# A decoder trunk in fp32r on one core: three weight pieces shared out anew, and a last half cut at 512, 384 and 128 columns

## The chip, the cores and the metric

The kernel runs on one core of a Trainium2 chip. The metric is the device time of one execution in microseconds; several runs are taken, and the median counts.

## What is computed

Two decoder layers over 256 tokens of width 1024, batch 1. Layer 0 has differential attention (8 heads, two score maps each), layer 1 attention over one block of shared keys and values (16 heads). Each attention and each MLP is followed by a layer norm of the scaled residual:

```python
def reference(x, ...):
    h = x
    for layer in range(DEPTH):                       # DEPTH = 2
        if layer < N_A_LAYERS:                       # layer 0
            mix = diff_attention(h, w_in_a[layer], ..., rel_bias, diff_lambda_init(layer))
        else:                                        # layer 1
            mix = moba_attention(h, w_q_b[j], w_out_b[j], kv[0], kv[1], kv[2], rel_bias)
        h = layer_norm(DEEPNORM_ALPHA * h + mix, ln1_g[layer], ln1_b[layer])
        h = layer_norm(DEEPNORM_ALPHA * h + squared_relu_mlp(h, w_up[layer], w_down[layer]),
                       ln2_g[layer], ln2_b[layer])
    return h
```

## The kernel before

Every large product is made of fp32r matmuls. A float32 operand is split into a high part, its fp32r rounding, and a low part, the rest; a product is then three matmuls, high x high, high x low and low x high (`three`, lines 141 to 147). Each has a weight load of its own.

The weights lie in DRAM as 96 *units* of 128 x 2048, in the order of use, and come in two *pieces* of 1024 columns each. A piece passes three queues: SyncE issues its load (`fetch`, line 90), ScalarE makes the high part `whi` (`head`, line 103, one piece ahead), VectorE the low part `wlo` (`piece`, line 115), and once VectorE has read a piece, the load of the one five further on may be issued into its buffer. `bg(n, True)` puts n pieces into the queues at the place in the program where it stands; `bg(n)` without `True` only as many as a credit allows that grows with the matmuls. `unit(u)` asks for a unit before its matmuls and puts in what is missing. The order of instructions on each engine is the order of the program text, and each engine works through its queue in that order.

The change touches three places.

*The end of attention 0* (`attention`, the branch `if diff`, lines 644 to 694). When the last scores are turned (`turn(7)`, `turned(7)`), heads 4 to 7 are multiplied with V (`values`), the heads of group 0 are transposed into `act` (`o_turn(0, h)`), the output projection runs in eight parts (`mix(h, c, ks)`: h is the half of 128 tokens, c the half of 512 columns, ks the heads, `G0` the first four and `G1` the last four), and between them group 4 is scaled by its rms norm (`rms(4, ...)`, line 584) and transposed (`o_turn(4, h)`, line 292). Of each transposed block ScalarE writes `act_hi` (line 72) and VectorE `act_lo` (line 76 with a scale, line 74 without). `mix(h, c, G1)` reads both. Then VectorE adds the residual and takes the statistics (`ln_add`, lines 310 and 312) and norms (`ln_apply`, lines 318 to 331); TensorE transposes the normed half (`ln_turn`, line 292), and the first MLP reads its high and low part (lines 141 to 143).

Ten pieces stand in this stretch, in groups of 2, 3, 2, 1 and 2 between the steps just told.

*The last half of the last MLP* (`mlp`, lines 896 to 906). The tokens of half 1 get their last two of eight chunks of the down projection column block by column block, so that VectorE can add and take statistics of one block while TensorE is in the next. The blocks are 512, 256 and 256 columns; the two narrow ones go to banks of their own (`rest`). For each block there are 8 x 3 matmuls. `step=256` is the width over which one statistics instruction goes.

*The last norm* (`ln_apply`, lines 314 to 333, with `each`). After the aggregate (line 318) VectorE finds 1/sqrt with small instructions between which the four centrings of 256 columns stand (line 321), then scales four times 256 columns (line 330), and each is stored by a DMA of 128 KB that SyncE issues (line 878). The same function, with 512 columns at a time, serves all other norms; there the list of its blocks is the same after the change.

Of the kernel before, what the change touches and what calls it, by code (L numbers as in the profile page):

```python
# [29 lines left out]
D = 1024  # L30
# [22 lines left out]
def trunk(ctx: ExitStack, tc: tile.TileContext, x, first, units, lam_a, subln, rel_bias,  # L53
# [53 lines left out]
    def piece():  # L107

        while state["head"] < state["piece"] + 1 + LEAD and head():
            pass  # L110
        v, s = divmod(state["piece"], PER)
        if state["piece"] == state["head"]:
            return False
        c = slice(s * PIECE, (s + 1) * PIECE)
        nc.vector.tensor_tensor(split[v][1][:, c], raws.pop(state["piece"]), split[v][0][:, c].bitcast(F32),  # L115
                                op=ALU.subtract)
        fetch(state["piece"] + RAWS)
        state["piece"] += 1
        return True

    def bg(most=8, force=False):

        while most > 0 and (force or state["credit"] >= 1.0 / PER):
            if not piece():
                state["credit"] = min(state["credit"], 1.0)
                return
            state["credit"] -= 1.0 / PER
            most -= 1
# [176 lines left out]
    def ln_add(h, c0, c1, mix, alpha=ALPHA, step=512):  # L305

        if c0 == 0:
            stats[h] = small.tile([P, D // step, 6], F32, name=f"st{step}")
        xh = xres[:, h]
        nc.vector.scalar_tensor_tensor(xh[:, c0:c1], xh[:, c0:c1], alpha, mix, op0=ALU.mult, op1=ALU.add)  # L310
        for c in range(c0, c1, step):
            nc.vector.bn_stats(stats[h][:, c // step], xh[:, c:c + step])

    def ln_apply(i, h, chunk, each=None):

        xh = xres[:, h]
        mv = small.tile([P, 2], F32, name="mv")
        nc.vector.bn_aggr(mv, stats.pop(h).rearrange("p a b -> p (a b)"))

        def centred(s):  # L320
            return lambda: nc.vector.scalar_tensor_tensor(xh[:, s], xh[:, s], mv[:, 0:1], lnp[i][:, 0, s],
                                                          op0=ALU.subtract, op1=ALU.mult)

        ahead = D if each else chunk
        r = rsqrt(mv[:, 1:2], 1, fill=[centred(slice(c, c + chunk)) for c in range(0, ahead, chunk)])
        for c in range(0, D, chunk):
            s = slice(c, c + chunk)
            if c >= ahead:
                centred(s)()
            nc.vector.scalar_tensor_tensor(xh[:, s], xh[:, s], r, lnp[i][:, 1, s],  # L330
                                           op0=ALU.mult, op1=ALU.add)
            if each:
                each(s)
# [4 lines left out]
    def attention(layer, u0):  # L338
# [4 lines left out]
        with tc.tile_pool(name=f"attn{layer}", bufs=2) as pool, \  # L343
# [4 lines left out]
            def v_out(c, h):  # L348
                nc.scalar.activation(V[:, h, c * 512:(c + 1) * 512], pv[c, h], AF.Copy)
# [158 lines left out]
            def turn(p):  # L508
                t, _ = T.pop(p)
                AT[p] = []  # L510
                for m in range(1 if diff else 2):
                    pt = bank("c")
                    for j in range(3):
                        k = (j + 2) % 3
                        nc.tensor.transpose(pt[:, j * P:(j + 1) * P], t[:, m, k * P:(k + 1) * P], ident)  # L515
                    AT[p].append(pt)

            def turned(p):
                a = pool.tile([P, len(AT[p]), 384], F32, name="aT", bufs=4 if diff else 2)
                for m, pt in enumerate(AT[p]):  # L520
                    src = pt[:, :384].rearrange("p (j t) -> p j t", j=3)
                    dst = a[:, m].rearrange("p (j t) -> p j t", j=3)
                    if diff:
                        nc.scalar.activation(dst, src, AF.Copy)
                    elif m == 0:
                        nc.scalar.activation(dst, src[:, :, ::-1], AF.Copy)
                    else:
                        nc.vector.tensor_copy(dst, src[:, :, ::-1])
                AT[p] = a
# [114 lines left out]
            if diff:  # L644
                turn(5)
                v_unit(u0 + 10, 1, 0)
                halves_hi(7)
                softmax_a(6)
                halves_lo(7)
                turned(5)  # L650
                scale = rms(0, [O[0][:, h] for h in range(2)], nc.gpsimd)
                bg(1)
                softmax_b(6)
                scores(7)
                turn(6)
                v_unit(u0 + 11, 1, 1)
                turned(6)
                softmax_a(7)
                bg(1, True)
                softmax_b(7)  # L660
                for h in range(2):
                    v_out(1, h)
                for h in range(2):
                    scale(h)
                turn(7)
                turned(7)
                for p in (4, 5, 6):
                    values(p, (0,))
                for p in (4, 5):
                    values(p, (1,))  # L670
                o_turn(0, 0)
                values(6, (1,))
                o_turn(0, 1)
                values(7)
                bg(2, True)
                mix(0, 0, G0)
                scale = rms(4, po, nc.vector)
                scale(0)
                scale(1)
                bg(3, True)  # L680
                mix(0, 1, G0)
                mix(1, 0, G0[:2])
                o_turn(4, 0)
                mix(1, 0, G0[2:])
                o_turn(4, 1)
                bg(2, True)
                for c in range(2):
                    mix(0, c, G1)
                    if c == 0:
                        bg(1, True)  # L690
                    ln_add(0, c * 512, c * 512 + 512, pw[0, c])
                ln_apply(layer, 0, 512)
                bg(2, True)
                mix(1, 1, G0)
            else:
                turn(5)
                mix(0, 0, G0[:2])
                values(4)
                turned(5)
                mix(0, 0, G0[2:])  # L700
                halves_hi(7)
                softmax_a(6)
                halves_lo(7)
                softmax_b(6)
                scores(7)
                values(5)
                turn(6)
                mix(0, 1, G0)
                softmax_a(7)
                turned(6)  # L710
                collect(4)
                bg(1, True)
                softmax_b(7)
                bg(1, True)
                values(6)
                mix(1, 0, G0)
                turn(7)
                turned(7)
                bg(2, True)
                mix(0, 0, G1[:2])  # L720
                values(7)
                collect(6)
                mix(0, 1, G1[:2])
                bg(1, True)
                for c in range(2):
                    mix(0, c, G1[2:])
                    ln_add(0, c * 512, c * 512 + 512, pw[0, c])
                ln_apply(layer, 0, 512)
                mix(1, 1, G0)
# [16 lines left out]
    def mlp(layer, u0, then):  # L746
# [3 lines left out]
        with tc.tile_pool(name=f"mlp{layer}", bufs=2) as pool:  # L750
            H, acc, rest, SQ = {}, {}, {}, {}
# [129 lines left out]
            if not last:  # L881
                for j in range(2):
                    down(6, j, (1,))
                bg(2, True)
                down(7, 0, (1,))
                ln_turn(0, 0)
                ln_turn(0, 1)
                bg(1, True)
                down(7, 1, (1,))
                ln_add(1, 0, 512, acc[1, 0])  # L890
                ln_add(1, 512, 1024, acc[1, 1])
                bg(1, True)
                ln_apply(i, 1, 512)
                then()
            else:
                xh = xres[:, 1]
                nc.vector.scalar_tensor_tensor(xh[:, 512:], xh[:, 512:], ALPHA, acc[1, 1], op0=ALU.mult, op1=ALU.add)
                for c0, c1 in ((0, 512), (512, 768), (768, 1024)):
                    for c in (6, 7):
                        for j in range(2):  # L900
                            down(c, j, (1,), ((c0, c1),))
                    if c0 == 0:
                        ln_add(1, c0, c1, acc[1, 0], step=256)
                    else:
                        ln_add(1, c0, c1, rest[c0][:, :c1 - c0], 1.0, 256)
                ln_apply(i, 1, 256, write(1))

    engines = {ET.PE, ET.Activation, ET.DVE, ET.Pool, ET.SP}
# [78 lines left out]
```

## Time and profile before

| | before |
|---|---|
| median of 3 runs | 593.54 us (592.69 to 594.05) |
| the profiled execution | 593.64 us |
| its span | 591.6 us |
| TensorE busy | 579.4 us, 98% |
| VectorE busy | 378.0 us, 64% |
| ScalarE busy | 319.0 us, 54% |
| mean granted clock of TensorE | 0.996 of full speed |

The profile is that of one execution. The profiled execution is 2.0 us longer than its span; times within the trace count from the span's start. PE is TensorE's matmul side, PEld its weight loads, DVE is VectorE, ACT ScalarE, and SPq the queue of SyncE that issues the loads and stores. The end of a matmul is modelled, its start is recorded; so the pace of a row of matmuls is read from start to start.

### The profile page before, as it was taken

The page shows a single profiled execution, that of the slowest core. Times are in us where ns is not written, and L with a number is a line of the kernel's source. Part 1 is how long each engine was busy: PE and PEld are TensorE (multiplying, and loading weights), DVE is VectorE, ACT ScalarE, POOL GpSimd, SP SyncE. Part 2 cuts the span into 40 slices and gives each one's busy share as a digit, 9 for nine tenths or more (in the row PEclk, how much of TensorE's full clock was granted, in tenths as well). Part 3 has the DMA queues.
Part 4 walks back from the last instruction along what each step waited for, and adds up shares of the span by engine and source line. Part 5 has one row for each costly group of instructions (what it writes and reads, how often), then busy time and mean ns, then how long its engine had stood idle before and what let it go on. Part 6 is the DMA issues. An engine that isn't in the chain of part 4 may idle for free.

```text
span 591.6 us, 9650 instructions
## 1 busy us (share of the span) xinstructions
PE 579.4 (98%) x3768; PEld 514.8 (87%) x3768; DVE 378.0 (64%) x692; ACT 319.0 (54%) x540; POOL 12.8 (2%) x45
## 2 busy tenths in 40 slices
PE   8999998999999999999999999999999999999993
PEld 6999987889899899898889999878899899899883
DVE  5797769976743744553877777697785544554236
ACT  6676777458664655552446556542885564554100
POOL 2000020000000000000000000000000000000000
PEclk9999999999999999999999999999999999999998
DMA  8996735548756736746259744151798556553002
GB/s 295 333 351 201 242 127 165 206 151 298 242 184 214 263 137 241 247 159 201 79 171 319 279 145 166 55 178 36 238 331 284 174 184 214 184 173 107 1 0 71
DMA packets 35548, 113.03 MB, mean 191 GB/s; under 512 B 3872, under 2 KB 8880, under 8 KB 35504
## 3 DMA queue, kind: packets, MB, share of 16 engines
q1 hardware_dynamic: 34144, 107.95, 53.9%
q0 software_dynamic: 1152, 4.19, 2.3%
q8 instruction: 29, 0.48, 0.3%
q10 hardware_dynamic: 208, 0.29, 0.1%
q14 instruction: 15, 0.12, 0.1%
HBM read 111.35 MB, written 1.07 MB: 190 GB/s over the span
## 4 chain that ended last, share of the span: by engine, by line
PE 95%; DVE 2%; DMA 1%; ACT 1%; issue 0%; SPq 0%; DVEq 0%
PE ps_b L145 13%; PE ps_a L143 13%; PE ps_a L142 13%; PE ps_a L141 12%; PE ps_b L147 12%; PE ps_b L146 12%; PE ps_b L143 4%; PE ps_b L141 4%; PE ps_b L142 4%; PE ps_a L462 2%; PE ps_c L515 1%; PE ps_c L292 1%; DMA raw<-in_first 1%; PE ps_a L553 1%; PE ps_c L782 1%; PE ps_a L381 1%
## 5 line engine op out<-in xcount | busy, mean ns | idle before, releaser
L115 DVE TENSOR_TENSOR wlo<-raw,whi 128x1024 fp32r<-128x1024 f32 x188 | 222.4, 1220 | 60.2 <-ACT whi L103 59.9
L103 ACT ACTIVATE whi<-raw 128x1024 fp32r<-128x1024 f32 x188 | 190.1, 1053 | 74.3 <-PE ps_a L143 51.5
L145 PE MATMUL ps_b<-act_hi,whi 128*128 128x256 f32 x640 | 179.3, 280 | 0.0
L146 PE MATMUL ps_b<-act_lo,whi 128*128 128x256 f32 x640 | 177.2, 277 | 0.0
L147 PE MATMUL ps_b<-act_hi,wlo 128*128 128x256 f32 x640 | 177.2, 277 | 0.0
L145 PEld LDWEIGHTS ps_b<-act_hi,whi 128*128 128x128 f32 x640 | 120.2, 188 | 1.5 <-issue 0.7
L146 PEld LDWEIGHTS ps_b<-act_lo,whi 128*128 128x128 f32 x640 | 120.4, 188 | 0.6
L147 PEld LDWEIGHTS ps_b<-act_hi,wlo 128*128 128x128 f32 x640 | 120.3, 188 | 0.0
L143 PE MATMUL ps_a<-whi,h_lo 128*128 128x512 f32 x248 | 97.6, 394 | 0.0
L142 PE MATMUL ps_a<-wlo,h_hi 128*128 128x512 f32 x248 | 97.1, 392 | 0.0
L141 PE MATMUL ps_a<-whi,h_hi 128*128 128x512 f32 x248 | 96.7, 390 | 0.0
L74 DVE TENSOR_TENSOR h_lo<-sqr,h_hi 128x512 fp32r<-128x512 f32 x24 | 16.6, 693 | 77.2 <-ACT h_hi L72 77.2
L142 PEld LDWEIGHTS ps_a<-wlo,h_hi 128*128 128x128 f32 x248 | 46.6, 188 | 10.3
L141 PEld LDWEIGHTS ps_a<-whi,h_hi 128*128 128x128 f32 x248 | 46.6, 188 | 9.7
L143 PEld LDWEIGHTS ps_a<-whi,h_lo 128*128 128x128 f32 x248 | 46.6, 188 | 9.5
L759 ACT ACTIVATE relu<-ps_b 128x512 f32<-128x512 f32 x32 | 19.1, 596 | 65.6 <-PE ps_b L147 54.0
L482 ACT ACTIVATE t<-t,mx 128x256 f32<-128x256 f32 x64 | 28.4, 445 | 31.8 <-DVE mx L479 31.8
L143 PE MATMUL ps_b<-whi,act_lo 128*128 128x512 f32 x96 | 37.8, 394 | 1.7 <-DVE act_lo L76 1.7
L141 PE MATMUL ps_b<-whi,act_hi 128*128 128x512 f32 x96 | 39.2, 409 | 0.0
L142 PE MATMUL ps_b<-wlo,act_hi 128*128 128x512 f32 x96 | 37.5, 391 | 0.0
L141 PE MATMUL ps_a<-whi,act_hi 128*128 128x512 f32 x80 | 32.3, 404 | 0.0
L143 PE MATMUL ps_a<-whi,act_lo 128*128 128x512 f32 x80 | 31.3, 392 | 0.0
(140 smaller groups left out, 586.5 us busy)
## 6 DMA issues: line engine op xcount, KB each, us to landing
raw<-in_units SPq DMA_DIRECT2D x188, 512.0 KB, 4.5
bias<-scr SPq DMA_DIRECT2D x16, 256.0 KB, 5.2
lnp<-in_ln_g POOLq DMA_DIRECT2D x4, 512.0 KB, 4.4
lnp<-in_ln_b POOLq DMA_DIRECT2D x4, 512.0 KB, 5.7
raw<-in_first SPq DMA_DIRECT2D x5, 384.0 KB, 7.3
xres<-in_x SPq DMA_DIRECT2D x1, 1024.0 KB, 5.5
out<-xres SPq DMA_DIRECT2D x2, 256.0 KB, 2.1
out<-xres SPq DMA_DIRECT2D x4, 128.0 KB, 1.9
```

The costliest lines, as they stand in the source:

```text
L74: nc.vector.tensor_tensor(lo, src, hi.bitcast(F32), op=ALU.subtract)
L103: nc.scalar.activation(split[v][0][:, c], raws[state["head"]], AF.Copy)
L115: nc.vector.tensor_tensor(split[v][1][:, c], raws.pop(state["piece"]), split[v][0][:, c].bitcast(F32), op=ALU.subtract)
L141: nc.tensor.matmul(ps, a[0], w[0], start=start, stop=False)
L142: nc.tensor.matmul(ps, a[0], w[1], start=False, stop=False)
L143: nc.tensor.matmul(ps, a[1], w[0], start=False, stop=stop)
L145: nc.tensor.matmul(ps, w[0], a[0], start=start, stop=False)
L146: nc.tensor.matmul(ps, w[0], a[1], start=False, stop=False)
L147: nc.tensor.matmul(ps, w[1], a[0], start=False, stop=stop)
L462: nc.tensor.matmul(sc[m][:, c:c + n], a[r, q], b[r, :n], start=i == 0, stop=i == 2)
L482: nc.scalar.activation(t[:, m, s], t[:, m, s], AF.Exp, bias=mx[:, m, j:j + 1], accum_out=sm[:, m, j:j + 1])
L759: nc.scalar.activation(r, ps, AF.Relu)
```

## The change

```diff
--- before.py
+++ after.py
@@ -323,8 +323,8 @@
 
         ahead = D if each else chunk
         r = rsqrt(mv[:, 1:2], 1, fill=[centred(slice(c, c + chunk)) for c in range(0, ahead, chunk)])
-        for c in range(0, D, chunk):
-            s = slice(c, c + chunk)
+        for c, e in zip([0, *range(512, D, chunk)], [*range(512, D, chunk), D]):
+            s = slice(c, e)
             if c >= ahead:
                 centred(s)()
             nc.vector.scalar_tensor_tensor(xh[:, s], xh[:, s], r, lnp[i][:, 1, s],
@@ -664,6 +664,7 @@
                     scale(h)
                 turn(7)
                 turned(7)
+                bg(1, True)
                 for p in (4, 5, 6):
                     values(p, (0,))
                 for p in (4, 5):
@@ -677,7 +678,7 @@
                 scale = rms(4, po, nc.vector)
                 scale(0)
                 scale(1)
-                bg(3, True)
+                bg(1, True)
                 mix(0, 1, G0)
                 mix(1, 0, G0[:2])
                 o_turn(4, 0)
@@ -690,7 +691,7 @@
                         bg(1, True)
                     ln_add(0, c * 512, c * 512 + 512, pw[0, c])
                 ln_apply(layer, 0, 512)
-                bg(2, True)
+                bg(3, True)
                 mix(1, 1, G0)
             else:
                 turn(5)
@@ -895,14 +896,14 @@
             else:
                 xh = xres[:, 1]
                 nc.vector.scalar_tensor_tensor(xh[:, 512:], xh[:, 512:], ALPHA, acc[1, 1], op0=ALU.mult, op1=ALU.add)
-                for c0, c1 in ((0, 512), (512, 768), (768, 1024)):
+                for c0, c1 in ((0, 512), (512, 896), (896, 1024)):
                     for c in (6, 7):
                         for j in range(2):
                             down(c, j, (1,), ((c0, c1),))
                     if c0 == 0:
-                        ln_add(1, c0, c1, acc[1, 0], step=256)
+                        ln_add(1, c0, c1, acc[1, 0], step=128)
                     else:
-                        ln_add(1, c0, c1, rest[c0][:, :c1 - c0], 1.0, 256)
+                        ln_add(1, c0, c1, rest[c0][:, :c1 - c0], 1.0, 128)
                 ln_apply(i, 1, 256, write(1))
 
     engines = {ET.PE, ET.Activation, ET.DVE, ET.Pool, ET.SP}
```

In attention 0 the ten pieces are now in groups of 1, 2, 1, 2, 1 and 3: one is put in before `values`, two fewer stand between the scaling of group 4 and `o_turn(4, 0)`, and one more behind the norm of half 0. In the last half the blocks are 512, 384 and 128 columns, the statistics go over 128 columns, and the aggregate reads eight groups. In the last norm the centrings stay four of 256, the scalings and stores are one of 512 and two of 256 columns.

The order of VectorE's instructions at the end of attention 0, from the scaling of group 4 (line 584, `o`) over its low parts (line 76) to the first residual add, before:

```order
L584 TENSOR_TENSOR o<-ps_a,rs_y_1321 128x512 x2
L115 TENSOR_TENSOR wlo<-raw,whi 128x1024 x3
L76 SCALAR_TENSOR_TENSOR act_lo<-ps_c,gsub,act_hi 128x4x128 x2
L115 TENSOR_TENSOR wlo<-raw,whi 128x1024 x3
L310 SCALAR_TENSOR_TENSOR xres<-xres,ps_b 128x512
```

and now:

```order
L584 TENSOR_TENSOR o<-ps_a,rs_y_1325 128x512 x2
L115 TENSOR_TENSOR wlo<-raw,whi 128x1024
L76 SCALAR_TENSOR_TENSOR act_lo<-ps_c,gsub,act_hi 128x4x128 x2
L115 TENSOR_TENSOR wlo<-raw,whi 128x1024 x3
L310 SCALAR_TENSOR_TENSOR xres<-xres,ps_b 128x512
```

Two pieces have left the place ahead of the low parts. One of them now stands earlier, between the scaling of group 0 (the line 584 before this one) and its low parts.

The order of VectorE's instructions behind the norm of half 0, up to the low parts of the normed half (line 74) that the MLP reads, before:

```order
L330 SCALAR_TENSOR_TENSOR xres<-xres,rs_y_1440,lnp 128x512
L321 SCALAR_TENSOR_TENSOR xres<-xres,mv,lnp 128x512
L330 SCALAR_TENSOR_TENSOR xres<-xres,rs_y_1440,lnp 128x512
L115 TENSOR_TENSOR wlo<-raw,whi 128x1024 x2
L74 TENSOR_TENSOR act_lo<-ps_c,act_hi 128x4x128
L115 TENSOR_TENSOR wlo<-raw,whi 128x1024
L74 TENSOR_TENSOR act_lo<-ps_c,act_hi 128x4x128
```

and now:

```order
L330 SCALAR_TENSOR_TENSOR xres<-xres,rs_y_1434,lnp 128x512
L321 SCALAR_TENSOR_TENSOR xres<-xres,mv,lnp 128x512
L330 SCALAR_TENSOR_TENSOR xres<-xres,rs_y_1434,lnp 128x512
L115 TENSOR_TENSOR wlo<-raw,whi 128x1024 x3
L74 TENSOR_TENSOR act_lo<-ps_c,act_hi 128x4x128
L115 TENSOR_TENSOR wlo<-raw,whi 128x1024
L74 TENSOR_TENSOR act_lo<-ps_c,act_hi 128x4x128
```

The second of the two pieces now stands here, ahead of the first low part.

The order of VectorE's instructions in the last half, from its first block's add to the aggregate, now:

```order
L310 SCALAR_TENSOR_TENSOR xres<-xres,ps_a 128x512
L312 BN_STATS st_5981<-xres 128x6 x4
L310 SCALAR_TENSOR_TENSOR xres<-xres,ps_b 128x384
L312 BN_STATS st_5981<-xres 128x6 x3
L310 SCALAR_TENSOR_TENSOR xres<-xres,ps_b 128x128
L312 BN_STATS st_5981<-xres 128x6
L318 BN_AGGR mv<-st_5981 128x2
```

Before, the adds were 512, 256 and 256 columns wide, followed by two, one and one statistics instructions. On TensorE the 24 matmuls of the second block go from 256 to 384 columns and the 24 of the third from 256 to 128; their order is the same.

## Rows read from the trace of the kernel before

**Rows 1.** The page, busy time of each engine over the span: us, share, instructions

```profile
PE 579.4 (98%) x3768; PEld 514.8 (87%) x3768; DVE 378.0 (64%) x692; ACT 319.0 (54%) x540; POOL 12.8 (2%) x45
```

**Rows 2.** Waits of TensorE from 20 us on: us, times, longest

```profile
PE ps_b L143 <- DVE act_lo L76: 1.7, 1, 1.7
```

**Rows 3.** Timeline of VectorE, 88 to 101 us: start, us, operation [idle before <-releaser]

```profile
88.66 1.63 DVE L76 SCALAR_TENSOR_TENSOR act_lo<-ps_c,gsub,act_hi 128x512 fp32r<-128x512 f32 x2 [1.85 <-ACT act_hi L72]
...
96.53 3.48 DVE L115 TENSOR_TENSOR wlo<-raw,whi 128x1024 fp32r<-128x1024 f32 x3
99.93 1.40 DVE L76 SCALAR_TENSOR_TENSOR act_lo<-ps_c,gsub,act_hi 128x512 fp32r<-128x512 f32 x2
```

**Rows 4.** Timeline of TensorE at the wait

```profile
98.68 0.39 PE L142 MATMUL ps_b<-wlo,act_hi 128*128 128x512 f32 x1
100.73 0.50 PE L143 MATMUL ps_b<-whi,act_lo 128*128 128x512 f32 x1 [1.66 <-DVE act_lo L76]
```

**Rows 5.** Timeline of ScalarE, same stretch

```profile
87.93 0.69 ACT L72 ACTIVATE act_hi<-ps_c,gsub 128x512 fp32r<-128x512 f32 x1 [1.35 <-PE ps_c L292]
...
96.82 0.69 ACT L72 ACTIVATE act_hi<-ps_c,gsub 128x512 fp32r<-128x512 f32 x1 [0.52 <-PE ps_c L292]
98.64 0.69 ACT L72 ACTIVATE act_hi<-ps_c,gsub 128x512 fp32r<-128x512 f32 x1 [1.13 <-PE ps_c L292]
```

**Rows 6.** Timeline of VectorE, 111 to 124 us

```profile
111.95 2.35 DVE L115 TENSOR_TENSOR wlo<-raw,whi 128x1024 fp32r<-128x1024 f32 x2
114.22 0.68 DVE L74 TENSOR_TENSOR act_lo<-ps_c,act_hi 128x512 fp32r<-128x512 f32 x1
...
122.62 0.75 DVE L330 SCALAR_TENSOR_TENSOR xres<-xres,rs_y,lnp 128x512 f32<-128x512 f32 x1
```

**Rows 7.** Timeline of TensorE, 115 to 124 us

```profile
115.49 0.39 PE L143 MATMUL ps_b<-whi,act_lo 128*128 128x512 f32 x1
...
115.95 0.39 PE L142 MATMUL ps_b<-wlo,act_hi 128*128 128x512 f32 x1
...
123.97 0.60 PE L292 MATMUL ps_c<-ident,xres 128*128 128x128 f32 x4
```

**Rows 8.** Busy time by stretch: window, length, PE, PEld, DVE, ACT, POOL, PEclk, DMA share, GB/s

```profile
576.90:582.50 5.60, 5.60 (x50) 5.45 (x48) 3.83 (x8) 0.00 (x0) 0.00 (x0) 1.00 0.25 94
```

**Rows 9.** Timeline of TensorE, score matmuls of 128 columns (line 462)

```profile
379.73 0.27 PE L462 MATMUL ps_a<-kl,qh 64*128 64x128 f32 x2
379.84 0.27 PE L462 MATMUL ps_a<-kh,ql 64*128 64x128 f32 x2
```

**Rows 10.** Timeline of the weight loads after a 128-column matmul

```profile
65.75 0.19 PEld L145 LDWEIGHTS ps_b<-act_hi,whi 128*128 128x128 f32 x1
65.87 0.19 PEld L146 LDWEIGHTS ps_b<-act_lo,whi 128*128 128x128 f32 x1
```

**Rows 11.** Timeline of TensorE, f32 matmuls of 128 columns (lines 543, 544)

```profile
86.40 0.39 PE L543 MATMUL ps_a<-V,aT 128*128 128x128 f32 x2
86.63 0.39 PE L544 MATMUL ps_a<-V,aT 128*128 128x128 f32 x2
```

**Rows 12.** Groups by shape: busy us, mean ns of one | idle before

```profile
L103 ACT ACTIVATE whi<-raw 128x1024 fp32r<-128x1024 f32 x188 | 190.1, 1053 | 74.3 <-PE ps_a L143 51.5 <-DMA raw<-in_units 22.4
L310 DVE SCALAR_TENSOR_TENSOR xres<-xres,ps_b 128x512 f32<-128x512 f32 x4 | 2.7, 685 | 0.2
L310 DVE SCALAR_TENSOR_TENSOR xres<-xres,ps_b 128x256 f32<-128x256 f32 x2 | 0.8, 412 | 1.8 <-PE ps_b L143 1.8
L318 DVE BATCH_NORM_AGGREGATE mv<-st 128x2 f32<-128x24 f32 x1 | 0.3, 262 | 0.0
```

**Rows 13.** Timeline of VectorE and of the DMA queue of SyncE at the end

```profile
586.45 1.67 DVE L330 SCALAR_TENSOR_TENSOR xres<-xres,rs_y,lnp 128x256 f32<-128x256 f32 x4
586.96 0.33 SPq L878 DMA_DIRECT2D out<-xres  x1
588.35 0.40 SPq L878 DMA_DIRECT2D out<-xres  x1
```

## The prediction

> **What bounds the kernel now.** I read four views in this order: the page's busy times, the list of TensorE's waits, the timelines of three engines around the one long wait, and the timelines of the last 15 us. TensorE is busy for 98% of the span [rows 1], so a change counts only if it alters TensorE's own stream, a wait of TensorE, or what follows its last matmul. After the first 20 us the list of waits holds a single entry, 1.7 us, for `act_lo` from line 76 on VectorE [rows 2]. In the timeline line 143 starts at 100.73, 2.05 us after line 142 at 98.68, where 0.23 is the usual step (115.49 to 115.95 is two steps) [rows 4, 7]: 1.8 us are lost. Behind the last matmul VectorE works alone to the end of the last norm's scaling at 586.45 + 1.67 = 588.12, and the last store is issued at 588.35 [rows 13]. So two places matter: 98 us and the end.
>
> **The change part by part.** Sums are made against the profiled execution, 593.64 us (span 591.6); the median of the runs shown is 593.54, 0.1 below it.
>
> *The pieces in attention 0.* Before the wait VectorE does three weight pieces in a row (line 115, 96.53 to 99.93, 1.13 each) and only then the two line 76 instructions, 1.40 together [rows 3]; the wait ends with the first of them [rows 4]. The change leaves one piece there. Line 76 for the first half also needs `act_hi`, which ScalarE ends at 96.82 + 0.69 = 97.51 [rows 5]; so it runs at 97.66 to 98.36, before TensorE asks at 98.91. The wait is gone, 1.8 us. The piece that moves forward, to a place ahead of the 88.66 row, falls into 1.85 us in which VectorE sat idle, and the copy that ScalarE makes with it, 1.05 us long [rows 12], into 1.35 us of idle time [rows 3, 5]: I cost it at nothing. If its weights were late, these gaps would close first. The refill of its buffer goes to SP's queue earlier, none later than one piece's worth, and no TensorE wait names a weight piece [rows 2].
>
> But VectorE is the next to be late. The second line 76 now waits for ScalarE's second `act_hi`, 98.64 + 0.69 = 99.33 [rows 5], and ends near 99.37 + 0.74 = 100.11 instead of 99.93 + 1.40 = 101.33 [rows 3]: VectorE is 1.2 us ahead. From there to the first half's transposed norm it now has six pieces instead of five, three of them behind the norm. So line 74 there, which makes `act_lo` for the MLP, comes at 114.22 - 1.2 + 1.13 = 114.15 and ends at 114.83 [rows 6]. The first reader of it is TensorE's line 143, at 115.49 before [rows 7]; 1.8 us earlier would be 113.68, and it must wait until about 114.89. What is left of the 1.8 us is **0.6 us**. The next tight place says the same: the transposes at 123.97 read what line 330 ends at 122.62 + 0.75 = 123.37 [rows 6, 7], again 0.6 of room. Ends for this part: 0 (the whole gain eaten) and 1.8.
>
> *The last columns on TensorE.* 24 matmuls of 256 columns and 24 more become 24 of 384 and 24 of 128. The columns are the same 512, the instructions the same 48, at the full granted clock (1.00). The 48 now take 5.45 us, 0.1135 each [rows 8]; a 512-column one takes 0.23, so 384 columns lie at 0.171 and the first 24 at 4.10 us. For 128 columns with a fresh weight load each, the trace has the fp32r score matmuls of line 462: the first of one pair of terms starts at 379.73, that of the next at 379.84, 0.11 apart [rows 9], though 128 columns are half of 256. They run as two row halves at once, so I looked for a single load: behind a narrow f32 matmul the loads of lines 145 and 146 start 0.12 apart [rows 10]. A weight load seems to hold the loader for 0.11 whatever the matmul streams. I take 0.11: 24 x 0.11 = 2.64, together 6.74 against 5.45, **+1.3 us** on the path, since nothing but the end waits behind it. The ends: if the load could hide, a 128-column block would cost half a 256-column one, 0.057, and the sum is 5.47, +0.0; at the pace of an f32 matmul of 128 columns, two passes in 0.23 (86.40 to 86.63) [rows 11], it would be +4.1.
>
> The Trainium skill, TensorE: Matmul & The Clock Gate, section Back-to-back issue gap, gives about 81 ns per matmul for a sustained stream of loads and 128-column matmuls; with that figure the block of 24 is estimated at 1.94 us and the sum of the whole change at 593.2. Its rule speaks less against this change than the rows do, and no fp32r row here shows such a pace.
>
> *VectorE behind the last matmul.* The last residual add shrinks from 256 to 128 columns: 412 ns against 685 for 512 [rows 12] makes 0.27 per 256, so -0.14. The statistics of the last block shrink in the same way; I take the same -0.14. The aggregate reads 48 numbers instead of 24, which took 262 ns [rows 12]; between 0 and +0.26, I take +0.1, since much of so short an instruction is fixed. Together -0.18. The earlier statistics (four and three narrower ones) run while TensorE is in the next block and have over 1 us of room there: nothing.
>
> *Last step and stores.* Four scalings of 256, 0.4 us apart, become 512, 256, 256: 0.67 + 0.40 + 0.48 = 1.55 instead of 1.67. The end is set by SP, though: its four issues run from 586.96 to 588.35, 0.46 apart [rows 13], and the last norm result had been ready since 588.12. With three stores the first is issued at 586.45 + 0.75 + 0.03 = 587.23 and the third 0.93 later, at 588.16: -0.19. The last store is 128 KB as before, so its landing is unchanged. Bounds: -0.1 (only VectorE's part) and -0.25.
>
> Sum: -0.6 + 1.3 - 0.18 - 0.19 = +0.33 us, 593.97 against the profiled 593.64, 593.9 against the median. About 0.2% (1.2 us) is what a measurement of this kernel can tell from no change, so the forecast is **no change**, with the two halves of the edit working against each other.
>
> **The rivals.**
> 1. *The whole wait is won.* If the line 74 at 114.15 came sooner, or its reader later, the gain is 1.8 and the time 593.9 - 1.2 = 592.7. For it: VectorE's pieces behind the norm may start earlier if the norm does. Against: that norm chain starts where VectorE ends its pieces, not where TensorE ends, so its instructions stay in one queue. Chance 0.1.
> 2. *The narrow block costs its columns.* TensorE pays nothing, 593.9 - 1.25 = 592.65. For it: the columns are the same. Against: the 0.11 steps in two kinds of rows [rows 9, 10]. Chance 0.1. Both 1 and 2 would give 591.4.
> 3. *The narrow block streams at the f32 pace,* on the other side: a block of 128 columns loses the one-pass speed of fp32r and takes 0.23 per matmul. The point from which it decides is the width: all fp32r blocks with full weights in this trace have 256 columns or more, so only the 128-column block would pay. 24 x 0.12 = 2.9 more, 596.8. Against: the score matmuls are fp32r with 128 columns and start 0.11 apart, with half the rows [rows 9]. Chance 0.05.
> 4. *The forward move buys nothing,* because a later wait in the MLP or the next attention closes the 0.6: 594.5. Against: no other wait of TensorE in the list [rows 2]. Chance 0.1.
>
> **How the numbers follow.** The forecast has 0.65. The range from 592.6 to 594.8 takes in rivals 1, 2 and 4 and some 0.3 us of scatter; it leaves out rival 3 and the two gains together. Faster by over 0.2% (below 592.35) needs rivals 1 and 2 together, or one of them and scatter: 0.12. Slower by over 0.2% (above 594.73) needs rival 3, or rival 4 and scatter: 0.1. The rest, 0.78, is no change.
>
> **What would show it.** Right: no wait of 1.7 us at 98 us, and a new one of about 1.2 us at the first line 143 of the first MLP, for `act_lo` of line 74; the last 24 matmuls 0.11 us apart with loads just as far apart; three last stores, the last issued about 0.4 us sooner after the last matmul than before. Wrong: steps near 0.06 or 0.23 in the last 24 matmuls, no wait or another one behind 113 us, or a last store that lands later than 2 us behind its issue.

## The result and the profile after

| | before | changed |
|---|---|---|
| median | 593.57 us (592.69 to 594.05, 4 runs) | 599.57 us (599.22 to 599.96, 4 runs) |
| ratio to before | | 1.0108, 95% interval 1.0097 to 1.0120 |
| span of the profiled execution | 591.6 us | 597.6 us |

The change makes the kernel slower by 6.0 us. The forecast was no change at 593.9, with a range up to 594.8: it is wrong in sign and far out of its range.

The page of the changed kernel, which answers to [rows 1]: TensorE is busy for as large a share as before, with as many matmuls, but 7.3 us longer (586.7 against 579.4).

```profile
span 597.6 us, 9651 instructions
...
PE 586.7 (98%) x3768; PEld 519.9 (87%) x3768; DVE 378.4 (63%) x695; ACT 319.1 (53%) x540; POOL 12.9 (2%) x45
```

TensorE's waits in the changed kernel (engine, line and tile, what it waited for, us in total, times, longest), which answer to [rows 2]: the wait of 1.7 us on line 76 has gone, and one of 1.0 us on line 74 has come.

```profile
PE ps_c L186 <- DVE lnp L179: 1.2, 1, 1.2
PE ps_b L143 <- DVE act_lo L74: 1.0, 1, 1.0
PE ps_a L381 <- ACT whi L72: 0.4, 1, 0.4
```

So neither waits nor more work explain 6 us. To find where they arise I compared the starts of equal matmuls in the two traces. The changed kernel is 0.4 us ahead at 20 us and 0.6 at 60 us. (The 0.4 is scatter: e4 below, whose program differs from the one before only behind 570 us, is 0.6 ahead there. The other 0.2 comes in attention 0 in e1 too, whose tiles lie as in the changed kernel; why is open.) It is 1.3 ahead at 117 us, behind the new wait, and still 1.3 ahead at 150. Then it loses, with no gap anywhere: 2.1 behind at 316 us, 2.2 at 442, 5.3 at 577, when the last columns begin. The two stretches of loss, 3.4 and 3.1 us, are the two MLPs from their first down projection on. Together with 0.1 in between, **6.6 us** went in a stream of matmuls that never stops.

What changed there is the pace. TensorE's timeline of the kernel before, first and last of the 48 matmuls of a block of the down projection (512 columns) and of the 96 of the block of the up projection behind it (256 columns):

```profile
194.44 0.39 PE L141 MATMUL ps_a<-whi,h_hi 128*128 128x512 f32 x1
...
205.20 0.39 PE L143 MATMUL ps_a<-whi,h_lo 128*128 128x512 f32 x1
205.43 0.28 PE L145 MATMUL ps_b<-act_hi,whi 128*128 128x256 f32 x1
...
216.22 0.28 PE L147 MATMUL ps_b<-act_hi,wlo 128*128 128x256 f32 x1
```

And of the changed kernel: the first two up blocks of this MLP, between which its first down block lies, and the same two blocks as above:

```profile
138.01 0.28 PE L145 MATMUL ps_b<-act_hi,whi 128*128 128x256 f32 x1
...
148.79 0.28 PE L147 MATMUL ps_b<-act_hi,wlo 128*128 128x256 f32 x1
...
160.50 0.28 PE L145 MATMUL ps_b<-act_hi,whi 128*128 128x256 f32 x1
...
171.69 0.28 PE L147 MATMUL ps_b<-act_hi,wlo 128*128 128x256 f32 x1
...
194.25 0.39 PE L141 MATMUL ps_a<-whi,h_hi 128*128 128x512 f32 x1
...
205.16 0.39 PE L143 MATMUL ps_a<-whi,h_lo 128*128 128x512 f32 x1
205.38 0.28 PE L145 MATMUL ps_b<-act_hi,whi 128*128 128x256 f32 x1
...
216.57 0.28 PE L147 MATMUL ps_b<-act_hi,wlo 128*128 128x256 f32 x1
```

47 steps of the down block take 10.76 us before and 10.91 now: 228.9 and 232.1 ns each. 95 steps of the up block take 10.79 and 11.19: 113.6 and 117.8 ns. The up block ahead of the first down block still goes at 10.78 / 95 = 113.5, the next one at 11.19 / 95 = 117.8. In the first MLP 384 down matmuls lose 3.1 ns and 480 up matmuls 4.2, together 3.2 of the 3.4 us; the other 0.2 falls on matmuls right behind them. Nothing in the instructions has changed there: the same lines, shapes and order, at the full granted clock (1.00 in both).

No other engine does it either. Near the end of the second MLP there are 10 us in which TensorE works alone: VectorE, ScalarE and GpSimd are at 0.00, and the DMA share is 0.00. Before, with the first and the last of 43 matmuls from these 10 us:

```profile
560.00:570.00 10.00, 10.00 (x45) 8.19 (x45) 0.00 (x0) 0.00 (x0) 0.00 (x0) 1.00 0.00 0
560.05 0.39 PE L142 MATMUL ps_a<-wlo,h_hi 128*128 128x512 f32 x1
...
569.66 0.39 PE L142 MATMUL ps_a<-wlo,h_hi 128*128 128x512 f32 x1
```

and in the changed kernel:

```profile
563.00:573.00 10.00, 10.00 (x45) 8.11 (x43) 0.00 (x0) 0.00 (x0) 0.00 (x0) 1.00 0.00 0
563.01 0.39 PE L142 MATMUL ps_a<-wlo,h_hi 128*128 128x512 f32 x1
...
572.77 0.39 PE L142 MATMUL ps_a<-wlo,h_hi 128*128 128x512 f32 x1
```

That is 9.61 / 42 = 228.8 ns before and 9.76 / 42 = 232.4 now: the loss of the down projection is there with nothing else running. For the up blocks, beside which transfers run, that is not shown.

What has changed is where tiles lie. `step=128` makes the statistics tile of that half eight groups wide instead of four: 192 B per partition in place of 96, and its pool holds two of them. So every tile laid out behind it in SBUF starts 192 B further on, `h_hi` and `h_lo` of the down projection among them. `act_hi`, `act_lo` and the weight pieces lie ahead of it and stay.

The end, as the trace of the changed kernel shows it. TensorE's timeline of the last columns, first and last rows of the block of 384 and of that of 128 (answers to [rows 8]):

```profile
582.30 0.34 PE L141 MATMUL ps_b<-whi,h_hi 128*128 128x384 f32 x1
...
586.35 0.34 PE L143 MATMUL ps_b<-whi,h_lo 128*128 128x384 f32 x1
586.52 0.22 PE L141 MATMUL ps_b<-whi,h_hi 128*128 128x128 f32 x1
586.58 0.28 PE L142 MATMUL ps_b<-wlo,h_hi 128*128 128x128 f32 x1
...
589.04 0.27 PE L143 MATMUL ps_b<-whi,h_lo 128*128 128x128 f32 x1
```

The weight loads of the narrow block start just as far apart as its matmuls:

```profile
586.52 0.19 PEld L142 LDWEIGHTS ps_b<-wlo,h_hi 128*128 128x128 f32 x1
586.63 0.19 PEld L143 LDWEIGHTS ps_b<-whi,h_lo 128*128 128x128 f32 x1
```

VectorE's timeline behind the last matmul, the changed kernel (its line 330 and the last stores answer to [rows 13]):

```profile
589.35 0.29 DVE L310 SCALAR_TENSOR_TENSOR xres<-xres,ps_b 128x128 f32<-128x128 f32 x1 [1.36 <-PE ps_b L143]
589.67 0.29 DVE L312 BATCH_NORM_STATS2 st<-xres 128x6 f32<-128x128 f32 x1
590.00 0.37 DVE L318 BATCH_NORM_AGGREGATE mv<-st 128x2 f32<-128x48 f32 x1
...
593.02 1.54 DVE L330 SCALAR_TENSOR_TENSOR xres<-xres,rs_y,lnp 128x512 f32<-128x512 f32 x3
```

and SyncE's queue, the three stores:

```profile
593.80 1.31 SPq L879 DMA_DIRECT2D out<-xres  x3
```

Before, the first of the 48 last matmuls started at 576.99 and the last residual add at 582.63, 5.64 later; now 582.30 and 589.35, 7.05 later: +1.41. From that add to the end of the span it was 591.6 - 582.63 = 8.97 and is 597.6 - 589.35 = 8.25: -0.72. The whole of it: -0.6 (up to 60 us) - 0.7 (the rest of attention 0) + 6.6 (pace) + 1.4 - 0.7 = 6.0.

### The profile page after: what moved, and what is told of

The parts are those of the page before. It is cut to its first block, busy times and chain, and to the rows that moved or that the text cites. A ratio compares the mean times of both kernels' runs of the same rounds, so it can differ in the third digit from the quotient of the medians.

```text
span 597.6 us, 9651 instructions
## 1 busy us (share of the span) xinstructions
PE 586.7 (98%) x3768; PEld 519.9 (87%) x3768; DVE 378.4 (63%) x695; ACT 319.1 (53%) x540; POOL 12.9 (2%) x45
## 4 chain that ended last, share of the span: by engine, by line
PE 95%; DVE 3%; DMA 1%; issue 0%; ACT 0%; SPq 0%; DVEq 0%
PE ps_b L145 13%; PE ps_b L146 12%; PE ps_b L147 12%; PE ps_a L141 12%; PE ps_a L143 12%; PE ps_a L142 12%; PE ps_b L143 4%; PE ps_b L141 4%; PE ps_b L142 4%; PE ps_a L462 2%; PE ps_c L515 1%; DVE wlo L115 1%; PE ps_c L292 1%; DMA raw<-in_first 1%; PE ps_a L553 1%; PE ps_c L783 1%
## 5 line engine op out<-in xcount | busy, mean ns | idle before, releaser
L147 PEld LDWEIGHTS ps_b<-act_hi,wlo 128*128 128x128 f32 x640 | 121.7, 190 | 0.0
L141 PE MATMUL ps_a<-whi,h_hi 128*128 128x512 f32 x248 | 98.0, 395 | 0.0
```

What stands on the lines that cost most here:

```text
L141: nc.tensor.matmul(ps, a[0], w[0], start=start, stop=False)
L147: nc.tensor.matmul(ps, w[1], a[0], start=False, stop=stop)
```

## The experiments

My theory: the 6.6 us come from the place of tiles alone; the edits of the program itself are worth what the prediction gave them. The rivals: the narrow last blocks or the pieces slow TensorE down in some other way, and the moved tiles are chance.

**Place and edits apart.** Four kernels.

e1: the kernel before with an unused tile of 192 B behind the statistics.

```diff
             stats[h] = small.tile([P, D // step, 6], F32, name=f"st{step}")
+            if step < 512:
+                small.tile([P, 48], F32, name="pad2", bufs=1)
```

> The kernel before with one edit: an unused tile of 192 bytes per partition behind the statistics tiles, so that every tile of the attentions and MLPs (V, t, aT, relu, sqr, h_hi, h_lo and so on) lies 192 bytes further on, exactly where it lies in the changed kernel; no instruction differs. Theory PLACE (the wider room of the statistics moved h_hi and h_lo, and the down matmuls that load them, with the up matmuls between them, run some 4 ns slower each): the lag of 6.6 us that the trace of after builds up between 150 us and the end of the second MLP comes back, 593.6 + 6.6 = about 600, and the 256-column steps in the MLPs are 117.8 ns instead of 113.4. Theory RHYTHM (the pieces that moved, or the waits that went, leave TensorE in a slower rhythm from then on; where tiles lie does not matter): 593.6, steps of 113.4 ns.

Measured: 599.58 us against 592.96, ratio 1.0116 (1.0099 to 1.0133). Steps in the MLPs: 117.8 and 232.2 ns. An unused tile does all of the harm.

e2: the changed kernel, with one buffer for its wide statistics tile, so that nothing moves.

```diff
-            stats[h] = small.tile([P, D // step, 6], F32, name=f"st{step}")
+            stats[h] = small.tile([P, D // step, 6], F32, name=f"st{step}",
+                                  bufs=2 if step == 512 else 1)
```

> The changed kernel with one edit: the 128-column statistics tile has one buffer instead of two (only one is ever used), so the pool has its old size and every tile of the attentions and MLPs lies where it lay before. All three parts of the change stay. PLACE: 599.6 - 6.6 = 593.0, between 592.5 and 594, steps in the MLPs 113.4 ns. RHYTHM: 599.6 as the changed kernel, steps 117.8 ns.

Measured: 593.16 us against 592.96, ratio 1.0005 (0.9996 to 1.0015). TensorE's timeline of the same two blocks as above:

```profile
192.66 0.39 PE L141 MATMUL ps_a<-whi,h_hi 128*128 128x512 f32 x1
...
203.41 0.39 PE L143 MATMUL ps_a<-whi,h_lo 128*128 128x512 f32 x1
203.65 0.28 PE L145 MATMUL ps_b<-act_hi,whi 128*128 128x256 f32 x1
...
214.44 0.28 PE L147 MATMUL ps_b<-act_hi,wlo 128*128 128x256 f32 x1
```

10.75 / 47 = 228.7 and 10.79 / 95 = 113.6 ns: the pace of before is back. Everything that the prediction costed is in this kernel, and it comes to +0.2 us (by the interval -0.2 to +0.9) where the prediction had +0.33.

e3: the sharing out of the pieces alone (the three `bg` lines of the change).

> The kernel before with the three moved pieces alone; end and norm as before, all tiles where they were. PLACE: only the 0.6 us of the attention, 593.0, a wait of about 1.0 us for act_lo of line 74 in the first MLP instead of the 1.7 us wait. RHYTHM: about 599, since the pieces alone make the rhythm.

Measured: 592.65 us against 592.96, ratio 0.9990 (0.9981 to 1.0000). In the trace TensorE gains 0.6 us through attention 0 and keeps it to the end; by the medians it is 0.3, which the interval (0.0 to 1.1 us) does not tell from 0.6. Its waits:

```profile
PE ps_b L143 <- DVE act_lo L74: 1.0, 1, 1.0
```

e4: the end alone (blocks, last norm and stores of the change, the wide statistics in one buffer as in e2).

> The kernel before with the end alone: blocks of 512, 384 and 128 columns, statistics over 128 columns (one buffer, so that no tile moves), scalings and stores of 512, 256 and 256. Both theories: TensorE's last 48 matmuls take 1.4 us more, what follows the last of them 0.7 us less, together 593.6 + 0.7 = 594.3; if the narrow end were what slows the rest, 599 or more.

Measured: 593.97 us against 592.96, ratio 1.0016 (1.0007 to 1.0026). +1.0 us, where the prediction's terms for it give 1.3 - 0.18 - 0.19 = +0.93.

These four settle where the time went. The rest ask what about the place it is.

**Which tile, and how far.** e5 is e1 with 128 B in place of 192.

```diff
+                small.tile([P, 32], F32, name="pad2", bufs=1)
```

> The kernel before with the unused tile behind the statistics at 128 bytes instead of the 192 of e1: the attention and MLP tiles lie 128 bytes further on than before. h_hi begins at byte 202496 of a partition, a multiple of 128 as before (202368), where it was 64 past one in e1. Theory HALF (what counts is in which half of 128 bytes a tile begins): as before, 593.0, MLP steps 113.5 and 229 ns. Theory ANY (another distance or a larger period counts, 256 bytes for instance): slow as e1, about 599, or something between.

Measured (2 runs): 598.5 us against 593.36, ratio 1.0089 (1.0070 to 1.0108). Down 233.3 ns; up blocks now at 113.5, now at 117.8, in turn.

e6 moves only `h_hi` and `h_lo`, by 192 B.

```diff
             def hidden(c):
+                pool.tile([P, 48], F32, name="padh", bufs=1)
```

> The kernel before with the 192 bytes put into the MLP's own pool ahead of h_hi: only h_hi and h_lo move; V, t, aT, relu and sqr, and the tiles of the attentions stay. If the weights of the down matmuls are what matters: slow as e1 in both MLPs, 599 to 600, MLP steps 117.8 and 232 ns, though the up matmuls between them read nothing that moved. If what ScalarE and VectorE read and write (relu, sqr) matters, or the attention's tiles: 593.0.

Measured (2 runs): 599.34 us against 593.36, ratio 1.0103 (1.0085 to 1.0122). Down 232.2; the up blocks 113.4 up to the one behind the first down, 117.8 from the next on. The tiles of the hidden layer are enough.

e7 moves only the weight pieces and the tiles just ahead of them (the residual and the identity among them), by 64 B.

```diff
-    small.tile([P, 24], F32, name="pad", bufs=1)
+    small.tile([P, 8], F32, name="pad", bufs=1)
...
+    const.tile([P, 16], F32, name="padc")
     xres = const.tile([P, 2, D], F32, name="xres")
```

> The kernel before with 64 bytes put in ahead of xres and 64 taken out behind the wide tiles: whi and wlo begin at a multiple of 128 bytes instead of 64 past one; act, h_hi and h_lo and all tiles of the attentions and MLPs stay. Theory ABSOLUTE (a tile that is loaded as weights must begin at a multiple of 128): as before in the down matmuls or faster in the up matmuls, 593.0 or less, since the up matmuls load whi and wlo. Theory PAIR (the two operands of one matmul must not begin in the same half of 128 bytes: before, h and act are at 0 and whi and wlo at 64; in e1 h is at 64 as whi and wlo are): now all are at 0, so both kinds of matmuls are slow, in the MLPs and in the attentions: 117.8 and 232 ns, 600 or more.

Measured (2 runs): 606.66 us against 593.36, ratio 1.0227 (1.0208 to 1.0245), the slowest of all. Down 232.4, up 119.4, and the projections of the attentions are slower too. So the tile that moves need not be `h`: a matmul's two operands count together.

**A period, or absolute places.** e9 is e1 with 256 B.

```diff
+                small.tile([P, 64], F32, name="pad2", bufs=1)
```

> As e5, with 256 bytes instead of 128 behind the statistics. HALF has fallen (e5 was slow with h_hi at a multiple of 128). Theory PERIOD 256 (what counts is where a tile begins within 256 bytes: act and h at 128, whi and wlo at 192 before): as before, 593.3, MLP steps 113.5 and 229 ns. Theory NEAR (every move of h_hi and h_lo away from where they were costs, for instance because a longer period than 256 counts): 598 to 600.

Measured: 593.48 us against 593.33, ratio 1.0001 (0.9990 to 1.0012); 228.9 and 113.6 ns. A move by 256 B costs nothing.

e10 is e1 with 64 B, which puts `h` on the same place modulo 256 as the weights.

```diff
+                small.tile([P, 16], F32, name="pad2", bufs=1)
```

> As e5, with 64 bytes: h_hi and h_lo begin at 192 within 256 bytes, the same as whi and wlo. The one place of the four that has not run (128 before, 64 in e1, 0 in e5). If only the distance of 64 that before has is good: slow, 598 to 600. If two operands at the same place are as good or better: 593 or less.

Measured: 595.57 us against 593.33, ratio 1.0033 (1.0014 to 1.0053), between the two times that were expected. TensorE's timeline of a down and an up block:

```profile
195.46 0.39 PE L141 MATMUL ps_a<-whi,h_hi 128*128 128x512 f32 x1
...
206.11 0.39 PE L143 MATMUL ps_a<-whi,h_lo 128*128 128x512 f32 x1
206.34 0.28 PE L145 MATMUL ps_b<-act_hi,whi 128*128 128x256 f32 x1
...
217.53 0.28 PE L147 MATMUL ps_b<-act_hi,wlo 128*128 128x256 f32 x1
```

The downs are faster than before (10.65 / 47 = 226.6 ns), but the ups behind them go at 117.8 (11.19 / 95), though their own operands have not moved. The time as a whole is worse.

e11 moves all wide tiles together by 64 B (a tile of 64 B ahead of `act_hi`).

```diff
+    const.tile([P, 16], F32, name="padc")
     act = (const.tile([P, NK, S], F32R, name="act_hi"), const.tile([P, NK, S], F32R, name="act_lo"))
```

> 64 bytes put in ahead of act_hi, so that all wide tiles, act, xres, raw, whi, wlo and those of the attentions and MLPs, move by the same 64 bytes and keep their distances. Theory ABSOLUTE (each tile has a good place within 256 bytes): slow as in e7, about 606, in attentions and MLPs. Theory DISTANCE (what counts is how far apart the weights and the moving operand of one matmul begin, taken within 256 bytes: 64 before, 128 in e1 and e7, 192 in e5): as before, 593.3.

Measured: 593.38 us against 593.33, ratio 1.0002 (0.9990 to 1.0013); 228.9 and 113.6. What counts is the distance between the tiles, not where they lie.

e12 puts `act`, the weights and `h` all on the same place modulo 256.

```diff
-    small.tile([P, 24], F32, name="pad", bufs=1)
+    small.tile([P, 40], F32, name="pad", bufs=1)
...
+    const.tile([P, 48], F32, name="padc")
     xres = const.tile([P, 2, D], F32, name="xres")
```

> Kernel before, with 192 B of unused room ahead of the residual and 64 B more behind it, so that act_hi and act_lo, the weights and h_hi and h_lo all start at 128 modulo 256: the distance from the weights to the moving operand is 0 in the up and in the down projections (before: 192 and 64). If distance 0 is the best for any width (as 226.7 ns per 512-column down matmul in e10 says): down 226.7, up 113.5, time 590 to 592, faster. If the up matmuls of 256 columns pay at distance 0, or keep the slower pace behind the down matmuls as they did in e10 (117.8): 1,920 up matmuls x 4.3 ns = 8 us more, less 3 from the down projections, 597 to 599. If the distance is not what counts but the absolute places are: the weights at 128 instead of 192 were never tried, so any pace may come out, most likely one between.

Measured: 602.42 us against 593.17, ratio 1.0156 (1.0139 to 1.0172). The timeline of a down and an up block:

```profile
197.38 0.40 PE L141 MATMUL ps_a<-whi,h_hi 128*128 128x512 f32 x1
...
208.06 0.39 PE L143 MATMUL ps_a<-whi,h_lo 128*128 128x512 f32 x1
208.29 0.28 PE L145 MATMUL ps_b<-act_hi,whi 128*128 128x256 f32 x1
...
219.68 0.28 PE L147 MATMUL ps_b<-act_hi,wlo 128*128 128x256 f32 x1
```

Down 10.68 / 47 = 227.2, up 11.39 / 95 = 119.9 ns. That is worse than both times that were expected: the ups pay 6.3 ns each, not 4.3. They pay ahead of the first down block too (119.9 there), so at distance 0 the loss is their own: what is good for a stream of 512 columns is bad for one of 256.

All of it in one table: the start of the tiles modulo 256 (from the compiled programs; high and low parts of one operand agree), the distance of the operand that streams from the one that is loaded, modulo 256 (down: weights less `h`; up: `act` less weights), and the mean step from start to start within the blocks of the first MLP, 160 to 300 us (without the steps behind a transposition).

```
kernel        act  weights   h  | down: distance, ns | up: distance, ns
before        128    192    128 |   64   228.9       |  192   113.6
e9 (+256)     128    192    128 |   64   228.9       |  192   113.6
e11 (all 64)  192      0    192 |   64   228.9       |  192   113.6
e10           128    192    192 |    0   226.7       |  192   117.8 (113.5 ahead of the first down)
after, e1     128    192     64 |  128   232.2       |  192   117.8 (113.5 ahead of the first down)
e6            128    192     64 |  128   232.2       |  192   116.9 (mixed)
e5            128    192      0 |  192   233.3       |  192   115.2 (113.5 and 117.8 in turn)
e7            128      0    128 |  128   232.4       |  128   119.4
e12           128    128    128 |    0   227.1       |    0   119.9
```

In the down projection one distance gives one pace, whatever lies where: 0, 64, 128, 192 give 227, 228.9, 232, 233 (192 in one kernel only), and the 10 us in which TensorE works alone have the same paces: 226.7 in e10 and e12, 228.9 in e9, 232.4 in e1, e6 and e7, 233.3 in e5. In the up projection 0 and 128 are slow from the start. 192 gives one of two paces, 113.5 or 117.8, and 113.5 in every block of the MLPs only where the downs between stand at 64; a distance of 64 there was not tried. Of the placements tried, none beats that of the kernel before.

**A version that beats both.** The prediction and e3 say that pieces in front of line 74 hold up the MLP. e8 moves one piece ahead of `values`, as the change does, and one not behind the norm but between the two low parts of group 4. It takes the change's last norm and stores, leaves the last columns at 512, 256 and 256, and moves no tile.

```diff
+                bg(1, True)
                 for p in (4, 5, 6):
...
-                bg(3, True)
+                bg(1, True)
                 mix(0, 1, G0)
                 mix(1, 0, G0[:2])
                 o_turn(4, 0)
+                bg(1, True)
                 mix(1, 0, G0[2:])
```

> A version meant to beat both: the kernel before, no tile moved, end blocks 512, 256 and 256 as before, scalings and stores 512, 256 and 256, and the pieces shared out in another way: one ahead of the values of head 4, one (not three) ahead of the first low part of line 76, one between the two low parts of line 76, where VectorE otherwise waits for ScalarE, and two behind the norm as before. VectorE then stays 1.1 us ahead up to line 74 in the first MLP, so both waits should go: -1.7 from the attention, -0.3 from three stores instead of four: 591.0 against 593.0. If a wait for act_lo at 113 us shows all the same, 592.0 to 592.7.

Measured: 591.04 us (590.51 to 591.53, 5 runs) against 593.36, ratio 0.9964 (0.9951 to 0.9978). Of TensorE's waits only the one at the start is left:

```profile
PE ps_c L186 <- DVE lnp L179: 1.2, 1, 1.2
```

VectorE's timeline, where line 74 now starts at 112.53, 0.8 us earlier than in the changed kernel (113.34, below):

```profile
110.26 2.35 DVE L115 TENSOR_TENSOR wlo<-raw,whi 128x1024 fp32r<-128x1024 f32 x2
112.53 0.68 DVE L74 TENSOR_TENSOR act_lo<-ps_c,act_hi 128x512 fp32r<-128x512 f32 x1
```

In this trace attention 0 gains 1.64 us, and from the last residual add to the end of the span it is 8.4 us (from 580.52) against 8.97. By the medians it is 2.3 us faster than the kernel before, which in turn is 6.0 faster than the changed one.

## Why the prediction was wrong, and where it was right

**The pieces in attention 0: right.** The prediction had the wait at 98 us gone, a new one at the first line 143 of the MLP for line 74, and 0.6 us left. VectorE's timeline of the changed kernel answers to [rows 3, 6]:

```profile
96.97 0.74 DVE L76 SCALAR_TENSOR_TENSOR act_lo<-ps_c,gsub,act_hi 128x512 fp32r<-128x512 f32 x1
98.68 0.75 DVE L76 SCALAR_TENSOR_TENSOR act_lo<-ps_c,gsub,act_hi 128x512 fp32r<-128x512 f32 x1 [0.97 <-ACT act_hi L72]
...
109.94 3.49 DVE L115 TENSOR_TENSOR wlo<-raw,whi 128x1024 fp32r<-128x1024 f32 x3
113.34 0.68 DVE L74 TENSOR_TENSOR act_lo<-ps_c,act_hi 128x512 fp32r<-128x512 f32 x1
```

and TensorE's first line 143 behind it:

```profile
114.08 0.51 PE L143 MATMUL ps_b<-whi,act_lo 128*128 128x512 f32 x1 [1.03 <-DVE act_lo L74]
```

The wait is 1.03 us where 1.2 was forecast, the net 0.6 to 0.7 in e3 and in the changed kernel. Three pieces ahead of line 74 (3.49 us) are what it waits for, and e8, with two, has no wait there: shown. Rivals 1 and 4 fall with this.

**The last columns on TensorE: right.** +1.3 forecast, +1.41 measured. The narrow block steps by 0.11 with its loads 0.11 apart; the block of 384 by 4.22 / 24 = 0.176 (582.30 to 586.52) instead of 0.171. So a matmul of 128 columns with a load of its own costs what one of 256 does, and rivals 2 (0.057) and 3 (0.23) fall.

Of the two figures of the Trainium skill, TensorE: Matmul & The Clock Gate, the 81 ns for a load and a 128-column matmul (section Back-to-back issue gap) are not what this kernel's fp32r stream does: 0.112 is measured. The Trainium skill, TensorE: Matmul & The Clock Gate, section LDWEIGHTS, gives a load's time as its columns divided by 1.2, by estimate 107 ns for 128; the loads start 0.11 apart, near that, though the profile lists each as 0.19 long.

**Behind the last matmul: right up to the last issue, wrong behind it.** -0.37 forecast, -0.72 measured. From the last residual add to the first scaling it is 3.67 against 3.82 (-0.15, forecast -0.18). From there to the last issue it is 1.69 (594.71 less 593.02) against 1.90 [rows 13] (-0.21, forecast -0.19). The rest, 0.35, lies between the last issue and the end of the span, 2.9 against 3.25 us. I had costed that at nothing, because the last store is the same. e8 and e3 repeat it, 2.9 with three stores and 3.25 with four. It is not the landing: the last store lands 1.93 us behind its issue before and 2.02 now, just over the 2 us that the prediction had named as a sign of being wrong. It is what follows, 1.3 us before and 0.9 now. At the program's end SyncE waits for the DMAs one after another (line 983, now 984). SyncE's waits for stores at the end (waiter, what it waited for, us in total, times, longest), before:

```profile
SPq L983 <- DMA out<-xres: 1.4, 1, 1.4
```

and now:

```profile
SPq L984 <- DMA out<-xres: 1.1, 3, 0.5
```

Before, the first of these waits for a store is for the last one, and seven more, some 0.06 us each (590.30 to 590.76), are gone through behind it. With three stores the wait for the last store is the last of the list, and the others are over by then (596.77, then the end as before). The trace of e8 has the same order as the changed kernel. So the gain comes from where the last store stands on that list, and the prediction had no term for it.

**The step that failed** is this one: "The earlier statistics (four and three narrower ones) run while TensorE is in the next block and have over 1 us of room there: nothing." As instructions they do cost nothing. But their tile is 96 B wider, twice, and that moved an operand of the 744 down matmuls of 512 columns: 6.6 us in e1 and in the trace of the changed kernel, where the sum had 0. The sum went over instructions, waits and queues, and no step of it asked which tiles change in size and what lies behind them. The list of rivals has no such case either, so no part of the range stood for it. With the tiles held in place (e2) the time is 593.16, inside the range. The kernel's text had a hint: line 64 allocates 96 B in that same pool, under the name `pad`, that nothing reads.

The Trainium skill, SBUF — State Buffer, section SBUF: two separate sides, says that on the engines' side only the port pair shared by VectorE and GpSimd causes contention and that TensorE never waits on anyone. The traces agree as far as other engines go: the 232.4 ns are there while no other engine runs (563 to 573 us). But TensorE's pace still changes by some 6 ns per matmul with the distance of its own two operands, and there the measurement decides. Why the distance counts is not shown: none of these runs sees inside the reads.

## What to carry to other kernels

An edit that changes a tile's size, type or number of buffers also moves every tile behind it: compare the addresses in the two compiled programs, and cost a move by anything but a multiple of 256 B as a risk of its own for every stream of matmuls whose operands it moves against each other. When a kernel that TensorE bounds gets slower with no new wait, measure the step from start to start in the same block of both traces, stage by stage; a loss spread evenly over a stage (here 1 to 6%) is a pace, and a control with an unused tile tells a place from an edit in one run. A gain that frees one reader moves work to the next one behind: count the pieces in front of each reader, not only of the late one.

## What the runs showed of the hardware that I had not expected

- In the MLPs the pace of fp32r matmuls with a load each depends on the distance, modulo 256 B, between the start of the streamed and of the loaded operand: 226.7 ns at 0, 228.9 at 64, 232.2 at 128 and 233.3 at 192 for 512 columns; 113.5 or 117.8 at 192 and some 119 to 120 at 0 and 128 for 256. Moving both together (e11) or one by 256 B (e9) changes nothing.
- The pace of one kind of block reaches into the next. With `h` moved (changed kernel, e1, e10), the up block ahead of the first down runs at 113.5 ns and all those behind at 117.8, though their own operands lie as before. In e5 the blocks alternate. Even a faster down (226.7, distance 0) leaves slower ups behind it. The first 96 projections of attention 1 with 256 columns do the reverse: 117.8 ns each before (from 316.84 us) and 113.5 in the changed kernel (from 318.95). Step by step these are two rhythms of the same instructions: such a block starts at 116 to 119 ns in both kernels; in the fast ones the steps drop to 113 and 114 by the sixth and stay there, in the slow ones they never drop. It can happen at 512 columns too: 39 matmuls right behind the moved downs of the first MLP, whose own operands stand at 64 as before, take 233.3 ns in the changed kernel (from 295.89 us) and in e1, against 228.9 before. So the distance alone does not fix the pace of every block; what carries over is open.
- With one store fewer, the program ends 0.4 us sooner behind the last landing (0.9 against 1.3 us), because SyncE's waits for the other DMAs are then over when the last store lands.
